# The last SwiGLU on an undivided residual, and an output turned on TensorE

## The chip, the cores and the metric

The kernel runs on one core of one Trainium2 chip. The metric is the device time of one execution in microseconds (us). Engines are named as in the profile: PE is TensorE's matrix multiplication, PEld its weight loads, DVE is VectorE, ACT is ScalarE, SP is SyncE, whose queue issues nearly all DMAs here.

## The reference, cut to what matters

The program is a two-layer backbone over 256 latent tokens and 256 context tokens with 1024 features. Every sub-layer normalises, shifts and scales its input and adds a gated result to the residual. The change touches only the last sub-layer, a SwiGLU over the 256 latent tokens, and the final normalisation:

```python
def rmsnorm(x, g):
    return x * rsqrt(mean(x * x, axis=-1) + 1e-6) * g          # one 1/rms per token

def ffn_half_step(h, m, k, g, w_gate, w_up, w_down):
    shift, scale, gate = m[3 * k], m[3 * k + 1], m[3 * k + 2]   # one number per feature
    hn = rmsnorm(h, g) * (1 + scale) + shift
    return h + 0.5 * gate * ((silu(hn @ w_gate) * (hn @ w_up)) @ w_down)

lat = lat + m[5] * (mixer_output @ w_out)     # end of the odd mixer
lat = ffn_half_step(lat, m, 2, ...)           # w_gate, w_up: 1024 x 2816; w_down: 2816 x 1024
return rmsnorm(lat, final_norm)               # (256 tokens, 1024 features)
```

Since 1/rms is one number per token r(t), hn @ w = r(t) * (x @ w) + shift @ w, where x is the residual times one factor per feature.

## The kernel before

Features lie on the 128 partitions and tokens along the free dimension: the residual `res` is 8 blocks of 128 features by 512 tokens (256 context, 256 latent; `LAT` is the second half). Every product is taken to nearly full precision from halves: `wload` brings a 128x1024 block of weights (512 KB) by a DMA on SP's queue into one of 4 `raw` buffers, ACT rounds it to the high half (L148), DVE subtracts to get the low half (L149), both into one of 4 `w` buffers, and `mm3` (L158, L159, L160) issues three matmuls for each of the contraction's 128-row blocks: high by high, high by low, low by high. Products go to 6 PSUM buffers of 512 columns (`pm`); 2 more (`ps`) serve statistics.

The program is written in order, and a list scheduler sets the order of each engine's queue ahead of time: it takes ready instructions by priority, by its own clock. `high_priority` puts a block's instructions some 100 places earlier, `keep` holds an order as written. On the chip each queue runs in that order: an instruction that waits holds up those behind it.

The stretch around the change runs in these steps:

- **End of the odd mixer.** DVE and ACT finish eight input blocks `os` of the output projection.
- **Output projection** (`out_proj`, which calls `down`): for each of 8 feature blocks, 24 matmuls of 256 columns; DVE adds the gated product to the residual (`residual`, L429), ACT squares it (L291) and DVE adds the square to `acc` (L292).
- **Norm** (`norm_proj` for one half): two matmuls sum `acc` over the partitions (L253), DVE finds 1/rms for 256 tokens, two to a partition (L260 to L269), two matmuls spread it over the partitions (L278), and for each feature block DVE multiplies the residual by 1/rms and by scale (L309), ACT adds the shift and writes the high half (L314), DVE writes the low half (L316). Only then can the block's matmuls begin.
- **SwiGLU** (`ffn`): 22 hidden blocks, each with 24 matmuls for the gate and 24 for the up product, all 256 columns wide; ACT takes silu from PSUM (L458), DVE multiplies with the up product (L459), and ACT and DVE split the result in halves (L164, L165). After 6, 14 and 22 hidden blocks `down` multiplies what there is with w_down and adds to the residual.
- **Output** (`final`): again sums, 1/rms and its spreading, then for each feature block one DVE instruction (L1266) and one DMA of 128 KB on SP's queue (L1269). The output leaves as [feature, token] and is turned on the host.

Of the kernel before, what the change touches and what calls it, by code (L numbers as in the profile page):

```python
# [9 lines left out]
F32 = mybir.dt.float32  # L10
F32R = mybir.dt.float32r
I32 = mybir.dt.int32
AF = mybir.ActivationFunctionType
ALU = mybir.AluOpType
# [4 lines left out]
P = 128  # L19
D = 1024  # L20
KT = D // P
NTOK = 256
T2 = 2 * NTOK
F = 2816
NF = F // P
CHUNKS = ((0, 6), (6, 14), (14, 22))
# [7 lines left out]
SOON = 100  # L34
# [13 lines left out]
CTX, LAT = (0, NTOK), (NTOK, T2)  # L48
# [17 lines left out]
class Builder:  # L66
    def __init__(self, tc, ctx, t, out):
        self.tc, self.nc, self.t, self.out = tc, tc.nc, t, out
        pool = lambda name, bufs, **kw: ctx.enter_context(tc.tile_pool(name=name, bufs=bufs, **kw))
        self.cst = pool("cst", 1)  # L70
        self.rawp = pool("rawp", 4)
        self.wp = pool("wp", 4)
        self.sm = pool("sm", 4)
        self.pmm = pool("pmm", 6, space=PSUM)
        self.psm = pool("psm", 2, space=PSUM)
        self.dram = pool("dram", 1, space=DRAM)
        self.n = 0
        self.bg = []
        self.stage = None
        self.last_act = None  # L80
        self.keep = tc.keep_in_program_order

    def uid(self, s):
# [15 lines left out]
    def small(self, shape, tag, dt=F32, bufs=4):  # L99
        return self.sm.tile(shape, dt, tag=tag, name=self.uid(tag), bufs=bufs)  # L100
# [325 lines left out]
    def residual(self, i, ps, gate, h, last):  # L426
        c0, c1 = h
        r = self.res[:, i, c0:c1]
        self.nc.vector.scalar_tensor_tensor(  # L429
            r, ps[:, c0:c1], gate[:, i, VEC[h] : VEC[h] + 1], r, op0=ALU.mult, op1=ALU.add  # L430
        )
        if last:
            self.stat(i, h)


    def blocks(self, idx, n=3):
# [2 lines left out]
    def ffn(self, l, k, halves, after=None, spare=None, lead=None):  # L439
        nc, t = self.nc, self.t  # L440
        idx = 2 * l + k // 2
        lo, hi = halves[0][0], halves[-1][1]
        wgu = t["wgu"][idx]
        xs, pss = self.norm_proj(l, k, halves, self.blocks(idx, 4 if lead else 3), lead, spare if len(halves) > 1 else None)
        if lead is not None:
            self.mod_setup()
            self.start(self.mod_job((0, m) for m in (2, 3, 4, 5, 6, 7)), 1.6)
        for f0, f1 in CHUNKS:
            hid = []
            for f in range(f0, f1):  # L450
                for g in range(2):
                    if 2 * f + g == len(pss):
                        pss.append(self.pm())
                        w = self.wload(wgu[f, g], D)
                        self.mm3(pss[-1][:, lo:hi], self.wparts(w, KT), self.parts(xs, lo, hi))
                pg, pu = pss[2 * f : 2 * f + 2]
                s = self.slot("h", [P, 2, T2])
                nc.scalar.activation(s[:, 0, lo:hi], pg[:, lo:hi], AF.Silu)  # L458
                nc.vector.tensor_mul(s[:, 1, lo:hi], s[:, 0, lo:hi], pu[:, lo:hi])  # L459
                hd = self.slot("h", [P, 2, T2], F32R)  # L460
                self.split(hd[:, 0, lo:hi], hd[:, 1, lo:hi], s[:, 1, lo:hi])
                hid.append(hd)
                self.tick(2)
            gate = self.need(l, 3 * k + 2)
            self.down(lambda i: t["wd"][idx, i][:, f0 * P : f1 * P], hid, gate, halves, f1 == NF, f1 - f0, after)

    def proj(self, name, blk, xs, c0, c1):
        w = self.wload(self.t[name][blk], D)
        ps = self.pm()
        self.mm3(ps[:, c0:c1], self.wparts(w, KT), self.parts(xs, c0, c1))  # L470
        return ps
# [630 lines left out]
    def odd_mixer(self):  # L1102
        nc, t = self.nc, self.t
# [4 lines left out]
        xs, pss = self.norm_proj(1, 1, both, [t["od_in"][i] for i in ODD], spare="g")  # L1108
# [8 lines left out]
        for i in range(4):  # L1117
            ps = pss[i]
# [17 lines left out]
        for i in range(4):  # L1136
            ps = self.proj("od_in", 16 + i, xs, *LAT)
            nc.scalar.activation(lg[:, i], ps[:, N:T2], AF.Gelu_apprx_tanh)
        gates = {}
        for i in range(4):  # L1140
# [3 lines left out]
            for d in range(2):  # L1144
                ra = gates[i, d] = self.slot("g", [P, 2, T2])
                for g in range(2):
                    ps = self.pm()
# [100 lines left out]
        for i in range(4):  # L1248
            ps = self.pm()
            for f in range(4):  # L1250
                src = (yr if f < 2 else yi)[:, f % 2, i * P : (i + 1) * P]
                nc.tensor.matmul(ps[:, :N], lhsT=src, rhs=idft[:, f, :], start=f == 0, stop=f == 3)
            z = self.slot("hy", [P, N])
            v.scalar_tensor_tensor(z, uu[:, i], hb[:, i : i + 1], ps[:, :N], op0=ALU.mult, op1=ALU.add)
            v.tensor_mul(z, z, x0[:, i])
            o = self.slot("x", [P, 2, T2], F32R)
            self.split(o[:, 0, N:T2], o[:, 1, N:T2], z)
            os.append(o)
        self.out_proj("od_out", 1, os, [LAT])

    def final(self):
        nc = self.nc
        self.rb[LAT] = self.rstd([self.acc[LAT]], self.inv_d)
        for i in range(KT):
            y = self.slot("h", [P, NTOK])
            nc.vector.scalar_tensor_tensor(  # L1266
                y, self.res[:, i, NTOK:T2], self.gain[:, 6, i : i + 1], self.rb[LAT], op0=ALU.mult, op1=ALU.mult
            )
            nc.sync.dma_start(self.out[i], y)  # L1269

    def build(self):
        nc, t = self.nc, self.t
        both = [CTX, LAT]
        self.acc, self.rb, self.mod = {}, {}, {}
        self.res = self.const([P, KT, T2], "res")
        s5p = dict.fromkeys(("sb0", "sb1", "pa", "pb", "bank", "tm", "mb", "mbt", "vt", "et"), 1)
        self.phase(x=8, **s5p, gs=2, sc=1, junk=1, m=2, ct=1, h=10)
        self.ct = self.slot("ct", [P, KT, 32])
        for i in range(0, KT, 2):
            nc.sync.dma_start(self.res[:, i : i + 2, :], t["xt"][:, i : i + 2, :])  # L1280
            if i == 0:
                nc.sync.dma_start(self.ct, t["ct"])
                s5 = self.s5_prepare()
                next(s5)
        nc.scalar.activation(self.ct, self.ct, AF.Silu)
        invs = []
        for n, nm in ((D, "inv_d"), (384, "inv_q"), (256, "inv_kv")):
            tl = self.const([P, 1], nm)
            nc.gpsimd.memset(tl, 1.0 / n)
            invs.append(tl)  # L1290
        self.inv_d, self.inv_q, self.inv_kv = invs
        small = lambda: [
            setattr(self, nm, self.const(shape, nm, t[nm]))
            for nm, shape in (("sel", [P, 2]), ("ident", [P, P]), ("modb", [P, 2, 9, KT]), ("gain", [P, 7, KT]), ("sig", [P, 3]))
        ]
        self.mw0, self.w0 = [], []
        for i in range(KT):
            if i == 6:
                w = self.slot("sc", [P, 2, 4, 2 * P])
                self.mw0.append([w[:, r] for r in range(2)])  # L1300
            else:
                self.mw0.append([self.slot("m" if i == 5 else "h", [P, 4, 2 * P]) for _ in range(2)])
            for r in range(2):
                nc.sync.dma_start(self.mw0[i][r], t["modw0"][i, :, r])
            if i == 0:
                small()
            if i < 2:
                self.w0 += [self.wload(t["wgu"][0, i, g], D) for g in range(2)]
        with self.tc.high_priority(offset=SOON):
            for i in range(KT):  # L1310
                for h in both:
                    self.stat(i, h)
        for m in range(2):
            self.mod[0, m] = self.const([P, KT, 2], f"mraw0_{m}")
        self.start(s5, 2.5)
        self.ffn(0, 0, both, t["ev_in"][EVEN[0]], lead=self.mod_first)
        self.drain()
        self.phase(x=10, hh=2, p=5, c=5, v=2, kr=1, q=8)
        self.even_mixer()
        self.phase(x=8, sc=1, junk=1, m=3, y=7, h=10)  # L1320
        self.mod_setup()
        self.start(self.mod_job(((0, 8),) + tuple((1, m) for m in range(9))), 0.8)
        self.start(self.hyena_prepare(), 0.5)
        self.ffn(0, 2, both, t["wgu"][2, 0, 0], "y")
        self.need(1, 1)
        self.ffn(1, 0, both, t["od_in"][ODD[0]], "h")
        self.drain()
        self.phase(x=8, g=8, lx=2, hy=13)
        self.odd_mixer()
        self.phase(x=8, h=10)  # L1330
        self.ffn(1, 2, [LAT])
        self.final()
        self.stage.close()

# [158 lines left out]
```

## Time and profile before

| | |
|---|---|
| median of 3 runs | 1797.6 us (1797.04 to 1797.97) |
| the profiled execution | 1795.22 us, its span 1793.4 us |
| PE busy | 1727.7 us, 96% of the span |
| PEld, DVE, ACT busy | 81%, 70%, 38% |
| mean granted clock of TensorE | 0.986 of full speed |
| DMA | 292.63 MB, mean 163 GB/s |
| chain that ended last | PE 87%, DVE 7%, DMA 2% |

The span is the time from the first to the last event of one profiled execution; 1.82 us lie around it. [...] PE's records are longer than the distance between their starts, since matmuls overlap: the pace is read from starts.

### The profile page before, as it was taken

The page shows a single profiled execution, that of the slowest core. Times are in us where ns is not written, and L with a number is a line of the kernel's source. Part 1 is how long each engine was busy: PE and PEld are TensorE (multiplying, and loading weights), DVE is VectorE, ACT ScalarE, POOL GpSimd, SP SyncE. Part 2 cuts the span into 40 slices and gives each one's busy share as a digit, 9 for nine tenths or more (in the row PEclk, how much of TensorE's full clock was granted, in tenths as well). Part 3 has the DMA queues.
Part 4 walks back from the last instruction along what each step waited for, and adds up shares of the span by engine and source line. Part 5 has one row for each costly group of instructions (what it writes and reads, how often), then busy time and mean ns, then how long its engine had stood idle before and what let it go on. Part 6 is the DMA issues. An engine that isn't in the chain of part 4 may idle for free.

```text
span 1793.4 us, 24725 instructions
## 1 busy us (share of the span) xinstructions
PE 1727.7 (96%) x9364; PEld 1444.7 (81%) x9364; DVE 1252.9 (70%) x2464; ACT 684.1 (38%) x1082; POOL 13.2 (1%) x47
## 2 busy tenths in 40 slices
PE   5999999999989999999999999999999999789997
PEld 3778777779868788778888888888888888589997
DVE  7999999987488668776666686544543576875555
ACT  4433333343445653222222233222122357554442
POOL 0000000000000000000000000000000000000000
PEclk9999999999998999999999999999999999799999
DMA  9566666652465453464454544555433225146552
GB/s 324 173 216 211 223 214 216 210 189 90 125 185 172 120 189 115 154 223 152 147 183 153 164 130 130 179 173 163 156 117 95 94 94 201 49 150 191 183 185 92
DMA packets 108055, 292.63 MB, mean 163 GB/s; under 512 B 21216, under 2 KB 36448, under 8 KB 107680
## 3 DMA queue, kind: packets, MB, share of 16 engines
q1 hardware_dynamic: 102368, 287.39, 49.8%
q10 hardware_dynamic: 4928, 2.10, 0.7%
q8 instruction: 73, 1.20, 0.3%
q0 software_dynamic: 640, 1.57, 0.3%
q14 instruction: 46, 0.38, 0.1%
HBM read 272.20 MB, written 18.28 MB: 162 GB/s over the span
## 4 chain that ended last, share of the span: by engine, by line
PE 87%; DVE 7%; DMA 2%; ACT 1%; issue 1%; SPq 1%; DVEq 0%; ACTq 0%
PE mm L158 25%; PE mm L160 25%; PE mm L159 25%; PE mm L155 6%; DVE w L149 1%; DMA h<-in_modw_dram 1%; PE mm L1148 1%; SPq L981 1%; DVE nt L309 1%; DMA x<-d_g 1%; DVE x L316 1%; DMA x<-d_v 0%; PE ps L278 0%; PE ps L631 0%; PE ps L1059 0%
## 5 line engine op out<-in xcount | busy, mean ns | idle before, releaser
L159 PE MATMUL mm<-x,w 128*128 128x512 f32 (+1 forms) x1600 | 575.1, 360 | 0.0
L160 PE MATMUL mm<-x,w 128*128 128x512 f32 (+1 forms) x1600 | 574.5, 360 | 0.0
L158 PE MATMUL mm<-x,w 128*128 128x512 f32 (+1 forms) x1600 | 569.4, 361 | 4.5 <-ACT x L314 3.3
L148 ACT CAST w<-raw 128x1024 fp32r<-128x1024 f32 (+2 forms) x324 | 328.5, 1018 | 527.7 <-issue 254.1
L149 DVE TENSOR_TENSOR w<-raw,w 128x1024 fp32r<-128x1024 f32 (+2 forms) x324 | 384.0, 1187 | 191.7 <-ACT w L148 190.8
L158 PEld LDWEIGHTS mm<-x,w 128*128 128x128 f32 x1600 | 300.9, 189 | 55.9 <-ACT x L314 3.9
L159 PEld LDWEIGHTS mm<-x,w 128*128 128x128 f32 x1600 | 301.8, 189 | 48.9 <-issue 2.0
L160 PEld LDWEIGHTS mm<-x,w 128*128 128x128 f32 x1600 | 301.8, 189 | 48.7 <-issue 1.2
L225 DVE CUSTOM_DVE_ANT_0 junk<-m,sc 128x1024 f32<-128x1024 f32 x224 | 273.3, 1220 | 1.8 <-DMA m<-in_modw_dram 0.2
L158 PE MATMUL mm<-h,w 128*128 128x512 f32 (+1 forms) x632 | 229.2, 367 | 0.0
L160 PE MATMUL mm<-h,w 128*128 128x512 f32 (+1 forms) x632 | 228.4, 364 | 0.0
L159 PE MATMUL mm<-h,w 128*128 128x512 f32 (+1 forms) x632 | 228.3, 363 | 0.0
L429 DVE SCALAR_TENSOR_TENSOR res<-mm,mraw,res 128x256 f32<-128x256 f32 x192 | 86.1, 480 | 103.7 <-PE mm L160 92.8
L459 DVE TENSOR_TENSOR h<-h,mm 128x512 f32<-128x512 f32 (+1 forms) x88 | 54.6, 621 | 128.5 <-PE mm L160 111.0
L458 ACT ACTIVATE h<-mm 128x512 f32<-128x512 f32 (+1 forms) x88 | 48.0, 545 | 234.5 <-PE mm L160 223.7
L159 PEld LDWEIGHTS mm<-h,w 128*128 128x128 f32 x632 | 119.1, 188 | 20.6 <-issue 1.0
L158 PEld LDWEIGHTS mm<-h,w 128*128 128x128 f32 x632 | 118.6, 188 | 21.0 <-issue 1.1
L160 PEld LDWEIGHTS mm<-h,w 128*128 128x128 f32 x632 | 118.9, 188 | 20.5 <-issue 0.6
L155 PE MATMUL mm<-x,w 128*128 128x256 f32 x384 | 66.1, 289 | 6.7 <-DVE x L316 6.2
L314 ACT ACTIVATE x<-nt,mraw 128x256 fp32r<-128x256 f32 x88 | 42.9, 506 | 54.5 <-DVE nt L309 54.5
L155 PEld LDWEIGHTS mm<-x,w 128*128 128x128 f32 x384 | 53.9, 188 | 11.6 <-DVE x L316 9.2
L165 DVE TENSOR_TENSOR h<-h,h 128x512 fp32r<-128x512 f32 (+1 forms) x88 | 54.5, 619 | 0.0
(345 smaller groups left out, 1604.5 us busy)
## 6 DMA issues: line engine op xcount, KB each, us to landing
raw<-in_wgu_dram SPq DMA_DIRECT2D x176, 512.0 KB, 3.8
m<-in_modw_dram SPq DMA_DIRECT2D x130, 512.0 KB, 4.3
raw<-in_wd_dram SPq DMA_DIRECT2D x64, 512.0 KB, 3.6
raw<-in_wd_dram SPq DMA_DIRECT2D x32, 384.0 KB, 3.3
raw<-in_od_in_dram SPq DMA_DIRECT2D x20, 512.0 KB, 3.5
h<-in_modw_dram SPq DMA_DIRECT2D x12, 512.0 KB, 9.9
raw<-in_ev_in_dram SPq DMA_DIRECT2D x10, 512.0 KB, 3.5
d_mb<-mbt SPq DMA_DIRECT2D x16, 256.0 KB, 2.9
```

The lines of the kernel that those rows point to most:

```text
L148: nc.scalar.copy(hi[:, :n], raw[:, :n])
L149: nc.vector.tensor_sub(lo[:, :n], raw[:, :n], hi[:, :n])
L155: mm = lambda *a, **k: self.keep(self.nc.tensor.matmul(*a, **k))
L158: mm(ps, lhsT=wh, rhs=xh, start=first and i == 0, stop=False)
L159: mm(ps, lhsT=wh, rhs=xl, start=False, stop=False)
L160: r = mm(ps, lhsT=wl, rhs=xh, start=False, stop=last and i == n - 1)
L165: self.nc.vector.tensor_sub(lo, src, hi)
L225: nc.vector.tensor_tensor_reduce(self.junk, w, self.sc[:, v, :], 1.0, 0.0, ALU.mult, ALU.add, raw[:, dt, v : v + 1])
L314: self.last_act = nc.scalar.activation(x[:, 0, c0:c1], y, AF.Identity, bias=b)
L429: self.nc.vector.scalar_tensor_tensor(r, ps[:, c0:c1], gate[:, i, VEC[h] : VEC[h] + 1], r, op0=ALU.mult, op1=ALU.add)
L458: nc.scalar.activation(s[:, 0, lo:hi], pg[:, lo:hi], AF.Silu)
L459: nc.vector.tensor_mul(s[:, 1, lo:hi], s[:, 0, lo:hi], pu[:, lo:hi])
```

## The change

`ffn_last` takes the place of `ffn` for the last SwiGLU, without `norm_proj`. Its input tiles `xl` hold the residual times the factor per feature, not divided by the rms, in halves, and two more columns that hold the shift. `unscaled` writes the two columns ahead of the output projection, and, through the hook `done` at the end of `residual`, the 256 others as each feature block of the residual is finished: one ACT and one DVE instruction each. Every gate and up matmul is 258 columns wide, so that column 256 of the product is shift @ w. As a product leaves PSUM, it is multiplied by 1/rms (`rb`, spread as before and copied to SBUF once) and gets column 256 as a bias. The gate product: a DVE copy of one column, a DVE multiply, silu with a bias on ACT. The up product: a DVE copy, a DVE multiply, one DVE instruction that adds the bias and multiplies by the gate. The split follows as before.

In the last `down`, the hook of `final_tiles` has ACT multiply each finished residual block by the final gain and TensorE turn it in two 128x128 transposes into 4 PSUM tiles, held from there on. `final` needs 1/rms as one number per partition then, so it is not spread: two DVE and two ACT instructions of 512 columns, each followed by a DMA of 256 KB, two on SP's queue and two on ACT's. The pools of the mixer are kept, with no new phase.

```diff
@@ residual
         if last:
             self.stat(i, h)
+            if self.done is not None:
+                self.done(i, h)
@@
+    def ffn_last(self, l, k, xs):
+        nc, t = self.nc, self.t
+        idx = 2 * l + k // 2
+        n = NTOK
+        with self.tc.high_priority(offset=SOON):
+            rb = self.slot("g", [P, n])
+            nc.scalar.copy(rb, self.rstd([self.acc[LAT]], self.inv_d))
+        gate = self.need(l, 3 * k + 2)
+        for f0, f1 in CHUNKS:
+            hid = []
+            for f in range(f0, f1):
+                pg, pu = self.pm(), self.pm()
+                for g, ps in enumerate((pg, pu)):
+                    w = self.wload(t["wgu"][idx, f, g], D)
+                    self.mm3(ps[:, : n + 2], self.wparts(w, KT), self.parts(xs, 0, n + 2))
+                b = self.small([P, 2], "bias")
+                s = self.slot("g", [P, 2, n])
+                nc.vector.tensor_copy(b[:, 0:1], pg[:, n : n + 1])
+                nc.vector.tensor_mul(s[:, 0, :], pg[:, :n], rb)
+                nc.scalar.activation(s[:, 0, :], s[:, 0, :], AF.Silu, bias=b[:, 0:1])
+                nc.vector.tensor_copy(b[:, 1:2], pu[:, n : n + 1])
+                nc.vector.tensor_mul(s[:, 1, :], pu[:, :n], rb)
+                nc.vector.scalar_tensor_tensor(s[:, 1, :], s[:, 1, :], b[:, 1:2], s[:, 0, :], op0=ALU.add, op1=ALU.mult)
+                hd = self.slot("x", [P, 2, T2], F32R)
+                self.split(hd[:, 0, n:T2], hd[:, 1, n:T2], s[:, 1, :])
+                hid.append(hd)
+            if f1 == NF:
+                self.done = self.final_tiles()
+            self.down(lambda i: t["wd"][idx, i][:, f0 * P : f1 * P], hid, gate, [LAT], f1 == NF, f1 - f0)
+
+    def unscaled(self, l, k, xs):
+        nc = self.nc
+        sh, sc = self.mod[l, 3 * k], self.mod[l, 3 * k + 1]
+        def done(i, h):
+            x, r, g = xs[i], self.res[:, i, h[0] : h[1]], sc[:, i, 0:1]
+            with self.tc.high_priority(offset=SOON):
+                nc.scalar.activation(x[:, 0, :NTOK], r, AF.Copy, scale=g)
+                nc.vector.scalar_tensor_tensor(x[:, 1, :NTOK], r, g, x[:, 0, :NTOK], op0=ALU.mult, op1=ALU.subtract)
+        for i, x in enumerate(xs):
+            self.split(x[:, 0, NTOK : NTOK + 2], x[:, 1, NTOK : NTOK + 2], sh[:, i, 0:1].to_broadcast([P, 2]))
+        return done
@@ odd_mixer
+        self.xl = [self.slot("hy", [P, 2, T2], F32R) for _ in range(KT)]
+        self.done = self.unscaled(1, 2, self.xl)
         self.out_proj("od_out", 1, os, [LAT])
+        self.done = None
+
+    def final_tiles(self):
+        nc = self.nc
+        self.fin = [[self.pm() for _ in range(2)] for _ in range(2)]
+        def done(i, h):
+            y = self.slot("g", [P, NTOK])
+            nc.scalar.activation(y, self.res[:, i, h[0] : h[1]], AF.Copy, scale=self.gain[:, 6, i : i + 1])
+            for j in range(2):
+                nc.tensor.transpose(self.fin[j][i // 4][:, i % 4 * P : (i % 4 + 1) * P], y[:, j * P : (j + 1) * P], self.ident)
+        return done
 
     def final(self):
         nc = self.nc
-        self.rb[LAT] = self.rstd([self.acc[LAT]], self.inv_d)
-        for i in range(KT):
-            y = self.slot("h", [P, NTOK])
-            nc.vector.scalar_tensor_tensor(
-                y, self.res[:, i, NTOK:T2], self.gain[:, 6, i : i + 1], self.rb[LAT], op0=ALU.mult, op1=ALU.mult
-            )
-            nc.sync.dma_start(self.out[i], y)
+        _, r = self.rstd_stats([self.acc[LAT]], self.inv_d)
+        for j in range(2):
+            for q in range(2):
+                y = self.slot("g", [P, T2])
+                if q:
+                    nc.scalar.activation(y, self.fin[j][q], AF.Copy, scale=r[:, j : j + 1])
+                else:
+                    nc.vector.tensor_scalar(y, self.fin[j][q], r[:, j : j + 1], None, op0=ALU.mult)
+                (nc.scalar if q else nc.sync).dma_start(self.out[j, :, q * T2 : (q + 1) * T2], y)
@@ build
         self.odd_mixer()
-        self.phase(x=8, h=10)
-        self.ffn(1, 2, [LAT])
+        self.ffn_last(1, 2, self.xl)
         self.final()
```

## Rows read from the trace of the kernel before

**Rows 1.** Page: busy time by engine, and the chain that ended last, by engine.
```profile
PE 1727.7 (96%) x9364; PEld 1444.7 (81%) x9364; DVE 1252.9 (70%) x2464; ACT 684.1 (38%) x1082; POOL 13.2 (1%) x47
...
PE 87%; DVE 7%; DMA 2%; ACT 1%; issue 1%; SPq 1%; DVEq 0%; ACTq 0%
```

**Rows 2.** Windows: stretch, its length, busy time by engine, clock, DMA share, GB/s.
```profile
1580.00:1600.00 20.00, 14.04 (x99) 13.49 (x98) 13.46 (x39) 7.98 (x13) 0.00 (x0) 0.83 0.28 94
1600.00:1620.00 20.00, 20.00 (x171) 20.00 (x170) 12.48 (x16) 11.38 (x18) 0.00 (x0) 1.00 0.53 168
...
1780.00:1794.00 14.00, 2.66 (x20) 2.16 (x18) 6.08 (x25) 0.42 (x1) 0.00 (x0) 0.72 0.23 76
```

**Rows 3.** Timeline of PE, last output projection to first SwiGLU: start, length, work, idle before.
```profile
1583.59 0.28 PE L160 MATMUL mm<-x,w 128*128 128x256 f32 x1
1586.68 0.58 PE L253 MATMUL ps<-inv_d,acc 128*128 128x1 f32 x4 [2.82 <-DVE acc L292]
...
1591.62 1.23 PE L158 MATMUL mm<-x,w 128*128 128x256 f32 x4 [1.11 <-ACT x L314]
```

**Rows 4.** Timeline of PE: 59 steps of 256 columns, across the first chunk's end.
```profile
1623.82 0.28 PE L158 MATMUL mm<-x,w 128*128 128x256 f32 x1
...
1630.82 0.28 PE L160 MATMUL mm<-h,w 128*128 128x256 f32 x1
```

**Rows 5.** Timeline of PE: 13 steps of 512 columns, an earlier SwiGLU.
```profile
1404.76 0.40 PE L159 MATMUL mm<-h,w 128*128 128x512 f32 x1
...
1407.77 0.40 PE L160 MATMUL mm<-h,w 128*128 128x512 f32 x1
```

**Rows 6.** Timeline of PE: two transposes (L1197) among matmuls, odd mixer.
```profile
1500.84 0.28 PE L158 MATMUL mm<-x,w 128*128 128x256 f32 x1
1500.96 0.38 PE L1197 MATMUL ps<-ident,hy 128*128 128x128 f32 x2
1501.09 0.37 PE L159 MATMUL mm<-x,w 128*128 128x256 f32 x1
1501.30 0.28 PE L160 MATMUL mm<-x,w 128*128 128x256 f32 x1
```

**Rows 7.** Groups by line and shape from 1590 to the end: busy, mean ns, idle before.
```profile
L159 PE MATMUL mm<-x,w 128*128 128x256 f32 x352 | 99.3, 283 | 0.0
...
L149 DVE TENSOR_TENSOR w<-raw,w 128x1024 fp32r<-128x1024 f32 x56 | 68.3, 1225 | 45.9 <-ACT w L148 45.9
...
L429 DVE SCALAR_TENSOR_TENSOR res<-mm,mraw,res 128x256 f32<-128x256 f32 x24 | 11.3, 481 | 16.4 <-PE mm L160 16.2
L459 DVE TENSOR_TENSOR h<-h,mm 128x256 f32<-128x256 f32 x22 | 9.3, 421 | 11.3 <-PE mm L160 6.0 <-ACT h L458 5.0 <-issue 0.3
...
L314 ACT ACTIVATE x<-nt,mraw 128x256 fp32r<-128x256 f32 x8 | 4.0, 507 | 7.7 <-DVE nt L309 7.7
```

**Rows 8.** Timeline of DVE: last residual of the output projection, and what follows.
```profile
1583.90 0.48 DVE L429 SCALAR_TENSOR_TENSOR res<-mm,mraw,res 128x256 f32<-128x256 f32 x1 [0.20 <-PE mm L160]
1584.98 1.23 DVE L149 TENSOR_TENSOR w<-raw,w 128x1024 fp32r<-128x1024 f32 x1 [0.59 <-ACT w L148]
```

**Rows 9.** Timeline of the end: last residual, the 8 output blocks, their DMA issues.
```profile
1781.37 0.48 DVE L429 SCALAR_TENSOR_TENSOR res<-mm,mraw,res 128x256 f32<-128x256 f32 x1 [1.39 <-PE mm L160]
...
1786.36 3.22 DVE L1266 SCALAR_TENSOR_TENSOR h<-res,gain,ps 128x256 f32<-128x256 f32 x8 [0.73 <-PE ps L278]
1786.87 3.78 SPq L1269 DMA_DIRECT2D out_dram<-h  x8
```

**Rows 10.** Windows of the end, columns as in the second group.
```profile
1790.00:1791.00 1.00, 0.00 (x0) 0.00 (x0) 0.00 (x0) 0.00 (x0) 0.00 (x0) 0.50 0.80 269
1791.00:1792.00 1.00, 0.00 (x0) 0.00 (x0) 0.00 (x0) 0.00 (x0) 0.00 (x0) 0.50 0.46 156
```

**Rows 11.** Groups by line and shape, whole kernel: DVE reading PSUM, 2 and 512 columns.
```profile
L260 DVE TENSOR_SCALAR rs_v<-ps 128x2 f32<-128x2 f32 x10 | 1.6, 160 | 7.1 <-PE ps L253 7.1
...
L1068 DVE TENSOR_SCALAR y<-ps,sig 128x512 f32<-128x512 f32 x1 | 0.8, 751 | 2.3 <-ACT y L1067 2.3
```

More of the change, by code (lines that the diff above doesn't have):

```diff
@@ L1258, in odd_mixer @@
             os.append(o)
+        self.xl = [self.slot("hy", [P, 2, T2], F32R) for _ in range(KT)]
+        self.done = self.unscaled(1, 2, self.xl)
         self.out_proj("od_out", 1, os, [LAT])
+        self.done = None
+    def final_tiles(self):
[7 more added lines that the diff above has]
+        return done
     def final(self):
         nc = self.nc
-        self.rb[LAT] = self.rstd([self.acc[LAT]], self.inv_d)
-        for i in range(KT):
-            y = self.slot("h", [P, NTOK])
-            nc.vector.scalar_tensor_tensor(
-                y, self.res[:, i, NTOK:T2], self.gain[:, 6, i : i + 1], self.rb[LAT], op0=ALU.mult, op1=ALU.mult
-            )
-            nc.sync.dma_start(self.out[i], y)
+        _, r = self.rstd_stats([self.acc[LAT]], self.inv_d)
[7 more added lines that the diff above has]
+                (nc.scalar if q else nc.sync).dma_start(self.out[j, :, q * T2 : (q + 1) * T2], y)
     def build(self):
@@ L1486 @@
         aps[name] = nc.dram_tensor(f"in_{name}_dram", a.shape, mybir.dt.from_np(a.dtype), kind="ExternalInput").ap()
-    out = nc.dram_tensor("out_0_dram", (KT, P, NTOK), F32, kind="ExternalOutput").ap()
+    out = nc.dram_tensor("out_0_dram", (2, P, D), F32, kind="ExternalOutput").ap()
     with tile.TileContext(nc, schedule_with_timeline_sim=True) as tc:
@@ L1491 @@
     got = r.results[0]["out_0_dram"]
-    return np.ascontiguousarray(got.reshape(D, NTOK).T).reshape(1, NTOK, D)
+    return np.ascontiguousarray(got).reshape(1, NTOK, D)
```

## The prediction

> **What bounds the kernel now.** I read the page first. PE is busy for 96% of the span and holds 87% of the chain that ended last [rows 1], so an edit pays where PE stands still or runs at the low clock, and costs where it gives PE more to do. The windows of the last stretch show two such places: 1580 to 1600, where PE is busy for 14.04 of 20 us at a mean clock of 0.83, and the end, where it has 2.66 us of work in 14 [rows 2]. Between them PE is busy throughout at full clock, with DVE at some 60% and the DMA engines at half [rows 2]: the SwiGLU itself is bound by the pace of matmuls.
>
> The pace comes from starts, not from the records. 59 steps of 256 columns take 7.00 us [rows 4], so one takes 0.1186 us. 13 steps of 512 columns take 3.01 us [rows 5], 0.2315 us each. The difference over 256 columns is 0.44 ns a column.
>
> The stall is read on PE's timeline. The last matmul of the output projection starts at 1583.59, so the next could have at 1583.71; the SwiGLU's first starts at 1591.62 [rows 3]. PE stands for 7.9 us but for the two small groups of the norm. From there the SwiGLU has 22 x 48 = 1056 gate and up matmuls (three groups of 352, of which one stands in [rows 7]) and 22 x 8 x 3 = 528 of `down`, 1584 in all. At 0.1186 us they take 187.9 us. They took 189.6: the residual add starts 0.31 us after its block's last matmul (1583.90 against 1583.59 [rows 3, 8]), so the very last started at 1781.06 [rows 9] and was through its step at 1781.18. The 1.7 us over are the low clock after the stall and the feature blocks that arrive one by one. Stall and slow start are 7.9 + 1.7 = 9.6 us: what the first half of the change can win.
>
> **What the change takes away and puts in its place, at the start.** The norm's chain (sums, 1/rms, spreading, three instructions per feature block) leaves PE's way, since the first matmuls need only the undivided residual. That gains up to 9.6 us. Against it:
>
> *Two columns more.* 1056 matmuls x 2 columns x 0.44 ns = 0.9 us. From below it is nothing, if the step of 256 is held by something other than columns; but 0.2315 is 1.95 times 0.1186, so columns set it. From above, no row has 257 to 511 columns; a step as long as that of 512 would add 0.113 us x 1056 = 119 us. I take 0.9, since the two forms lie on a line almost through zero.
>
> *Sums and spreading inside the stream.* They were in the stall; now their eight records push matmuls back. By the transposes below (0.11 us each) that is 0.9 us; by their own 0.58 us for four at the low clock [rows 3], 1.2. I take 0.9.
>
> *The last feature block.* After the projection's last matmul the residual add takes 0.48 us [rows 8], then ACT and DVE write the halves: 0.51 by L314, which also has a pointer operand [rows 7], and 0.48. With the hand-overs that is 1.6 us, and PE has the first seven feature blocks of the first product to do meanwhile, 21 x 0.119 = 2.5 us. But ACT begins a weight cast of about 1 us at the same instant (DVE, after its 0.48, waits 0.59 for it and then takes 1.23 for the low half [rows 8]); behind both, the halves come up to 2 us later. So 0 to 1.1 us. PE's queue also holds the sums: they wait for `acc`, which today keeps PE for 2.82 us [rows 3]; placed too early they hold up the matmuls behind them by up to that.
>
> *1/rms itself* comes about 7 us after the projection's end as it does now, and evictions wait for it. Six PSUM buffers hold six products, 6 x 24 x 0.1195 = 17 us of PE's work: hidden; were there two buffers, PE would wait for about 1.5 us.
>
> *The writes of `xl`* (8 ACT and 8 DVE) move into the projection, where DVE waits 0.20 us for PE and 0.59 for ACT in the block shown, and ACT longer [rows 8]: they fit into these waits, but nearly fill them. I take nothing. The 16 small writes of the shift, about 0.16 us each by the 2-column instruction [rows 11], could fall where DVE is finishing the mixer: 0 to 1.3 us.
>
> *Evictions.* DVE has for one hidden block now 2 x 1.225 + 0.42 + 0.42 = 3.3 us. A second multiply (0.42), a three-operand instruction (0.48) and two copies (0.16 each) make 4.5 [rows 7, 11]. PE needs 48 x 0.1195 = 5.7 us: covered by 1.2 us. ACT stays under 3 us. At a chunk's end the chain from the last product to the halves grows by about 0.7 us, and the four PSUM tiles held for the transposes leave two in the last `down`: 0 to 0.6 us.
>
> For all these waits (last feature block, sums, shift writes, chunk ends) the ends are 0 and 5.8 us; I take 1.1, near the low end, because the order is laid out by readiness and PE has other ready matmuls at each of them.
>
> **The end.** 16 transposes: 14 of them lie among the last block's matmuls. In the odd mixer two of them lengthen the time from 1500.84 to 1501.30 to 0.46 us, where two plain steps take 0.237 [rows 6]: 0.11 us each, 1.6 us for 14. The other two run while DVE works on 1/rms. [...]
>
> What is left is the tail after PE. Now 1/rms is there at 1785.6, spread by 1786.36, the first DMA is issued at 1786.87, and the data flow at 269 GB/s into the last window, which is used for about half [rows 9, 10]. After, spreading goes (0.7 us), and the first block of 512 columns takes 0.75 us [rows 11] instead of 0.48: the first issue is about 0.4 us sooner. The megabyte still needs 3.9 us at 269 GB/s, and the producers are quicker (two engines, 1.4 us against 3.2), so the gain lies between 0.4 and 1.0. I take 0.6. [...]
>
> **Sum.** 9.6 - 0.9 - 0.9 - 1.6 + 0.6 - 1.1 = 5.7 us. Against its own time the profiled execution would go from 1795.2 to 1789.5; the median of the runs shown is 2.4 us above that execution, so I predict 1797.6 - 5.7 = 1791.9.
>
> **Rivals.**
> 1. *PE waits inside the stream for what it waited for in the open.* Sums, spreading and the last feature block stand in PE's queue ahead of matmuls that could run. For it: `acc` comes 2.8 us late behind a weight cast [rows 3, 8]. Against: the block of seven ready feature blocks. With 2.8 + 1.1 us more the gain is about 2: 1795.6, no measurable change. Chance 0.16.
> 2. *A transpose costs its whole record.* Two merged records span 0.38 us [rows 6], at 0.11 apart 0.27 each; if a matmul had to wait out each, 14 x 0.16 = 2.2 us more: 1794.1. Against it stand the same rows. Chance 0.04. [...]
> 3. *DVE becomes the pace of the SwiGLU (slower).* In its queue each low half waits for ACT, 45.9 us over 56, 0.82 each [rows 7]. If these waits stay as they are, DVE needs 4.5 + 2 x 0.82 = 6.1 us a hidden block against PE's 5.7, 0.4 x 22 = 8.9 us: 1800.8. It decides once DVE's waits in a hidden block exceed 1.2 + 5.7/22 = 1.5 us. Against: a queue that falls behind finds its inputs ready, and 4 weight buffers give slack. Chance 0.07.
> 4. *258 columns cost more than two columns (slower).* From 5.7 / 1056 = 5.4 ns per matmul over the 0.88 the gain is gone; 10 ns would give 1802.5. No row speaks for it. Chance 0.05.
> 5. *Hardly any cost shows*: without waits and with a tail gain of 1.0 it is 7.2 us, 1790.4; with the two columns free 1789.5. That is within my forecast. A gain above 9 us would need the end of the mixer to be reordered for the better as well: 0.04.
>
> **How the numbers follow.** The forecast itself (a gain of 3.6 to 9 us) has 0.64. This kernel's measurement can tell 0.2%, 3.6 us. Faster: 0.64 + 0.04 = 0.68. Same: rivals 1 and 2, 0.20. Slower: rivals 3 and 4, 0.12. The range leaves out rivals 3 and 4 and the few per cent with a gain above 10: 1787.5 to 1797.5.
>
> **What the profile after would show.** No stall of PE between projection and SwiGLU and a clock of 1.00 there; matmul steps of 0.1195 us; records of L253 and L278 and of the transposes spaced by 0.11 us among matmuls, with no idle time ahead of them; DVE at 75 to 80% in the SwiGLU, still waiting for others; a tail of about 11.4 us from the last matmul instead of 12.2. The prediction is wrong if PE idles in front of sums, transposes or the last feature block by more than 2 us in all, or if the steps grow by over 3 ns.

## The result, and the profile after

The changed kernel takes 1769.2 us (median of 4 runs, 1767.26 to 1772.87) where the kernel before takes 1797.3 (1796.6 to 1797.97): a ratio of 0.9846, interval 0.9829 to 0.9863. The gain of 28 us is five times the forecast of 5.7, and lies outside the stated range. The page after:

```profile
span 1767.9 us, 24860 instructions
...
PE 1704.0 (96%) x9376; PEld 1444.1 (82%) x9376; DVE 1268.6 (72%) x2546; ACT 693.7 (39%) x1101; POOL 13.2 (1%) x47
```

PE has 12 instructions more than in [rows 1] and is busy 23.7 us less. That is the first sign that the gain is not the stall's 8 us: time in which PE stands still is no part of its busy time. Where it was won shows on PE's timeline. The transposes of the odd mixer (L1247 here, [rows 6] before) belong to code that nobody changed: they are PE's instructions 7,322 and 7,323, and the first 7,622, by tiles and shapes, stand in the same order in both kernels:

```profile
1209.65 0.39 PE L161 MATMUL mm<-x,w 128*128 128x512 f32 x1
...
1213.95 0.39 PE L159 MATMUL mm<-x,w 128*128 128x512 f32 x1
...
1477.41 0.38 PE L1247 MATMUL ps<-ident,hy 128*128 128x128 f32 x2
```

They start at 1477.41, not 1500.96: 23.55 us were won before anything that the diff names has run. The first two rows are 19 steps of 512 columns apart (a step is the time from one start to the next), 0.2263 us each, where [rows 5] gave 0.2315. Over all steps of 512 columns the means are 232.2 and 226.9 ns; 4,784 x 5.3 ns = 25.4 us. The 1,536 steps of 256 columns ahead of the last SwiGLU grow by 0.7 ns each, 1.1 us, which leaves 24.3.

The stretch of the change itself, on the same timeline:

```profile
1559.44 0.28 PE L161 MATMUL mm<-x,w 128*128 128x256 f32 x1
1559.56 0.28 PE L159 MATMUL mm<-hy,w 128*128 128x258 f32 x1
...
1566.94 0.28 PE L160 MATMUL mm<-hy,w 128*128 128x258 f32 x1
1567.05 0.50 PE L254 MATMUL ps<-inv_d,acc 128*128 128x1 f32 x4
1567.41 0.37 PE L161 MATMUL mm<-hy,w 128*128 128x258 f32 x1
...
1577.16 0.60 PE L279 MATMUL ps<-ident,rs_y 128*128 128x128 f32 x4
...
1577.72 0.28 PE L161 MATMUL mm<-hy,w 128*128 128x258 f32 x1
1578.68 0.39 PE L159 MATMUL mm<-hy,w 128*128 128x258 f32 x1 [0.68 <-DVE g L490]
...
1734.33 0.44 PE L1323 MATMUL mm<-ident,g 128*128 128x128 f32 x2 [1.89 <-ACT g L1321]
...
1741.80 0.28 PE L159 MATMUL mm<-x,w 128*128 128x256 f32 x1
1741.92 0.38 PE L1323 MATMUL mm<-ident,g 128*128 128x128 f32 x2
1742.06 0.37 PE L160 MATMUL mm<-x,w 128*128 128x256 f32 x1
1742.26 0.28 PE L161 MATMUL mm<-x,w 128*128 128x256 f32 x1
...
1748.19 0.44 PE L1323 MATMUL mm<-ident,g 128*128 128x128 f32 x2 [1.27 <-ACT g L1321]
```

The stall of [rows 3] is gone: projection and SwiGLU are one step apart (1559.44, 1559.56), and the sums at 1567.05 stand among matmuls without a wait. Two transposes lengthen two steps (1741.80 to 1742.26) to 0.46 us, as in [rows 6]. But two other pairs in the stream wait for ACT.

### The profile page after: what moved, and what is told of

Read it like the earlier page. It is cut to its first block, busy times and chain, and to the rows that moved or that the text cites. A ratio compares the mean times of both kernels' runs of the same rounds, so it can differ in the third digit from the quotient of the medians.

```text
span 1767.9 us, 24860 instructions
## 1 busy us (share of the span) xinstructions
PE 1704.0 (96%) x9376; PEld 1444.1 (82%) x9376; DVE 1268.6 (72%) x2546; ACT 693.7 (39%) x1101; POOL 13.2 (1%) x47
## 5 line engine op out<-in xcount | busy, mean ns | idle before, releaser
L160 PE MATMUL mm<-x,w 128*128 128x512 f32 (+1 forms) x1424 | 520.9, 366 | 0.1
L161 PE MATMUL mm<-x,w 128*128 128x512 f32 (+1 forms) x1424 | 520.1, 366 | 0.0
L159 PE MATMUL mm<-x,w 128*128 128x512 f32 (+1 forms) x1424 | 515.4, 367 | 3.6 <-ACT x L315 2.2
L159 PEld LDWEIGHTS mm<-x,w 128*128 128x128 f32 x1424 | 267.8, 189 | 49.3 <-ACT x L315 2.5
L160 PEld LDWEIGHTS mm<-x,w 128*128 128x128 f32 x1424 | 268.9, 189 | 44.5 <-issue 2.0
L161 PEld LDWEIGHTS mm<-x,w 128*128 128x128 f32 x1424 | 268.7, 189 | 43.7 <-issue 1.2
L159 PE MATMUL mm<-h,w 128*128 128x512 f32 x456 | 178.5, 395 | 0.0
L161 PE MATMUL mm<-h,w 128*128 128x512 f32 x456 | 177.1, 391 | 0.0
L160 PE MATMUL mm<-h,w 128*128 128x512 f32 x456 | 176.9, 390 | 0.0
L462 DVE TENSOR_TENSOR h<-h,mm 128x512 f32<-128x512 f32 x66 | 45.3, 687 | 107.6 <-PE mm L161 95.4
L461 ACT ACTIVATE h<-mm 128x512 f32<-128x512 f32 x66 | 39.5, 598 | 195.9 <-PE mm L161 185.2
L159 PEld LDWEIGHTS mm<-h,w 128*128 128x128 f32 x456 | 85.7, 188 | 18.8 <-issue 1.1
L160 PEld LDWEIGHTS mm<-h,w 128*128 128x128 f32 x456 | 85.7, 188 | 18.4 <-issue 1.0
L161 PEld LDWEIGHTS mm<-h,w 128*128 128x128 f32 x456 | 85.6, 188 | 18.4 <-issue 0.6
L159 PE MATMUL mm<-hy,w 128*128 128x258 f32 x352 | 99.4, 284 | 0.7 <-DVE g L490 0.7
L161 PE MATMUL mm<-hy,w 128*128 128x258 f32 x352 | 99.8, 284 | 0.0
L160 PE MATMUL mm<-hy,w 128*128 128x258 f32 x352 | 99.7, 284 | 0.0
```

The costliest lines, as they stand in the source:

```text
L159: mm(ps, lhsT=wh, rhs=xh, start=first and i == 0, stop=False)
L160: mm(ps, lhsT=wh, rhs=xl, start=False, stop=False)
L161: r = mm(ps, lhsT=wl, rhs=xh, start=False, stop=last and i == n - 1)
```

## Experiments

**Is it the change, or its addresses?** The change's new tag `bias` takes 4 tiles of 32 bytes from the pool of small tiles. The pools of `x`, `g`, `h` and `hy` lie above it and move up by 128 bytes (`x` from 97376 to 97504 within a partition), while `w` below stays at 53728 (the addresses that the two programs give their tiles). Theory: this shift shortens the step. Rival: the change does it, by its order. One kernel has the shift without the change, the other the change without the shift:

```diff
# pad128: before, in an unused tag of the small pool (1 and 2 tiles: pad32, pad64)
+        for _ in range(4):
+            nc.vector.memset(self.small([P, 2], "pad", bufs=4), 0.0)
# after_noshift: after, the bias in one more column of s (whose other uses end at n)
-                b = self.small([P, 2], "bias")
-                s = self.slot("g", [P, 2, n])
+                s = self.slot("g", [P, 2, n + 1])
+                b = s[:, :, n]
```

> The kernel before with four unused 32-byte tiles at the end of the small pool, which moves every tile of the later pools (x, h, g, hy and so on) up by 128 bytes, as the new bias tiles of the change do; the queues hold the same instructions in the same order, with four memsets of two columns more on DVE. Theory A (the addresses of the streamed tiles set the step of a matmul): the 512-column step falls from 232 ns to 227 and the time to 1772 to 1776. Theory B (something else of the changed program, or the scheduler): within 2 us of 1797, step 232.

> The changed kernel with the two bias columns kept in two more columns of the s tile instead of tiles of their own, so that all pools lie where they lay before the change. Theory A: the 512-column step is 232 ns again, and what is left is the gain of the changed instructions alone, 4 to 8 us: 1789 to 1794. Theory B: 1767 to 1772 as the changed kernel.

> The kernel before with one unused 32-byte tile: later pools move by 32 bytes. Theory A: the step may differ from 232 ns either way, and the time follows by 4850 matmuls of 512 columns times the difference. Theory B: within 2 us of 1797.

> The kernel before with two unused 32-byte tiles: later pools move by 64 bytes. Theory A: as for 32 bytes, and with the two others a row that shows from which offset on the step changes. Theory B: within 2 us of 1797.

| kernel | x - w, mod 256 bytes | step of 512 | step of 256 (`down`) | us | ratio to before |
|---|---|---|---|---|---|
| before | 128 | 232.2 ns | 118.7 ns | 1797.6 | 1 |
| pad32 | 160 | 234.0 | 117.3 | 1802.7 | 1.0025 (1.0016 to 1.0035) |
| pad64 | 192 | 233.1 | 113.3 | 1789.4 | 0.9956 (0.9942 to 0.997) |
| pad128 | 0 | 226.9 | 120.0 | 1774.0 | 0.9864 (0.985 to 0.9879) |
| after_noshift | 128 | 232.2 | 119.0 | 1796.5 | 0.999 (0.9981 to 1.0) |

128 bytes that nothing uses win 23.6 us; the change at the old addresses wins 1.1, which is no measurable change. The rival fell. But the theory's time for after_noshift, 1789 to 1794, was missed too: it left more to the change alone than the change wins there. "x - w, mod 256" is the distance from the weights to the stream, as the remainder after division by 256. The steps are means over all starts of a kernel's trace, gaps left out.

**What of the addresses?** step_map runs matmuls alone, with the stream and the weights each moved in steps of bytes, and nothing else of the reference's computation. The question is whether the address of the stream alone counts, or that of the weights with it.

> Matmuls alone: the kernel loads one block of streamed data and one of weights, then issues products of 24 matmuls as in the kernel (high by high, high by low, low by high, 8 blocks), with nothing else running, and steps the start of the streamed data through 16 offsets of 32 bytes and that of the weights through 0, 32, 128 and 256; first 512 columns, then 256. It leaves out the whole computation of the reference. [...] Theory N (the address of the stream alone): rows for different weight offsets are alike. [...]

It takes 949 us. Worked out from the starts, 43 steps a point:

```
stream - weights, mod 256     0      32     64     96    128    160    192    224
512 columns, ns a step     226.7  233.3  228.9  233.5  233.4  234.2  233.4  233.2
256 columns, ns a step     120.0  117.7  117.8  119.9  118.6  118.7  117.8  118.3
```

With the weights moved by 0, 32, 128 and 256 bytes (for 256 columns by 0 and 32) the same values come back at the same distances, to 0.3 ns in nearly all points (the largest difference is 1.1 ns), and they repeat after 256 bytes. So Theory N fell: with matmuls alone the step went with the distance between the two operands (226.7 ns for 512 columns at 0, 233.4 at 128), not with one address. Two kernels test that in place: both128 moves `w` and `x` together by 128 bytes, w128 moves `w` by 128 and `x` by 512.

```diff
# both128 and w128: before, a tile of 128 bytes below all pools
+        nc.vector.memset(self.const([P, 32], "padc"), 0.0)
# w128 as well: 384 bytes between w and x
+        nc.vector.memset(self.small([P, 96], "pad", bufs=1), 0.0)
```

> The kernel before with 128 unused bytes among the constants: weights and streamed tiles move up together by 128 bytes, so that the streamed tiles lie where they lie after the change and the weights do not. [...] Theory N: 227 ns, 1774 within 3.

> The kernel before with 128 unused bytes among the constants and 384 in the small pool: weights move by 128 bytes, streamed tiles by 512. [...] Theory N modulo 512: 232 ns and 1797 within 3.

One run each: both128 has the old distance and takes 1796.8 us, w128 adds 384 to the old remainder of 128, which makes 512 or a distance of 0, and takes 1774.3 (before on the same chip 1797.8). PE's timeline of both128, 18 steps:

```profile
1209.84 0.40 PE L158 MATMUL mm<-x,w 128*128 128x512 f32 x1
...
1214.04 0.40 PE L158 MATMUL mm<-x,w 128*128 128x512 f32 x1
```

and of w128, 19 steps:

```profile
1209.76 0.39 PE L159 MATMUL mm<-x,w 128*128 128x512 f32 x1
...
1214.06 0.39 PE L160 MATMUL mm<-x,w 128*128 128x512 f32 x1
```

0.2333 against 0.2263 us in these stretches, at addresses that both differ from those of before. Theory N had it the other way round, 227 ns for both128 and 232 for w128, and fell here too: for steps of 512 columns it is the distance.

**What does the change itself win?** Its halves one by one at the new addresses, beside pad128 and after once more, on one chip; end_half ran on another, and its ratio is to before there. start_half keeps the old `final`. end_half is pad128 with the new `final` and the hook. after_late issues each pair of transposes one feature block later.

```diff
# start_half: after, with final and the output as before
-            if f1 == NF:
-                self.done = self.final_tiles()
# end_half: pad128, in ffn
+            if f1 == NF and halves == [LAT]:
+                self.done = self.final_tiles()
# after_late
-            for j in range(2):
-                nc.tensor.transpose(...)        # of block i
+            ys.append(y)
+            if i:
+                turn(i - 1)
+            if i == KT - 1:
+                turn(i)
```

> The kernel before moved by 128 bytes, again, as the base for the three others on one chip: 1773 to 1775, 0.986 of the kernel before.

> The changed kernel, again. Theory S (beside the move, the change is worth what the prediction summed, less the waits that its trace shows): 4 to 6 us under the moved kernel before, so 1768 to 1770. Theory L (the move is all of it): within 1 us of the moved kernel.

> The changed SwiGLU with the end of the kernel before (1/rms spread, 8 DVE instructions and 8 DMAs, no transposes), at the moved place. Theory S: the stall of 9.6 us goes, 0.9 for sums and 0.3 to 0.9 for two columns come back: 6 to 8 us under the moved kernel, 1766 to 1768, so faster than the whole change, because 14 transposes and the waits for them (1.6 + 3.2 us) cost more than the shorter tail gives (1.8). Theory L: within 1 us of the moved kernel.

> The kernel before with four unused tiles of 32 bytes (so the phase pools stand 128 bytes higher, as in the changed kernel) and with the new end alone: y by row statistics, 16 transposes on TensorE, 1/rms as a per-partition factor, two DMAs; the SwiGLU is the old one, with the stall ahead of it. Theory (the step of 512 columns comes back with the 128 bytes, and the end costs what the two traces of the changed kernel with and without it differ by): against the padded kernel (1774.0) it is 1 to 4 us slower, some 1776 to 1778, with TensorE waiting for ScalarE's y in front of the transposes and a tail shorter by 1.5 to 2 us. Rival (the end costs nothing or gains, as the prediction had it without the waits: 14 transposes of 0.11 against a shorter tail): 1773 to 1774. Second rival (the end costs less at the head of a stalled stage, as the waits are hidden by the old layout of the stream): 1772 to 1774 with no idle time ahead of the transposes.

> The changed kernel with the two transposes of a feature block issued one block later, behind the matmuls of the next. If TensorE's waits for the final-gain tiles (1.9 and 1.3 us in the trace) are lost time, they go: 2.5 to 3.5 us under the changed kernel, 1765 to 1767. If they only moved a wait from elsewhere: within 1 us of it.

From PE's starts: "stall" is from the last matmul of the projection to the SwiGLU's first, "tail" from the start of its last to the span's end.

| us | stall | SwiGLU | tail | median | ratio to before |
|---|---|---|---|---|---|
| before | 8.03 | 189.43 | 12.39 | 1798.0 | 1 |
| pad128 (again) | 8.04 | 191.60 | 12.85 | 1774.0 | 0.9866 (0.9852 to 0.9879) |
| after (again) | 0.12 | 197.61 | 10.71 | 1768.7 | 0.9836 (0.9823 to 0.985) |
| start_half | 0.12 | 192.66 | 12.38 | 1765.8 | 0.9819 (0.9806 to 0.9833) |
| end_half | 8.24 | 199.14 | 10.70 | 1779.5 | 0.9896 (0.988 to 0.9913) |
| after_late | 0.12 | 197.63 | 10.69 | 1768.9 | 0.9841 (0.9827 to 0.9854) |

The first half wins 8.2 us against pad128, and the second loses: 5.5 alone (across two chips; 1 to 4 were expected), 2.8 on top of the first. after_late wins nothing back. In after PE waits twice for ACT within the stream, 1.9 and 1.3 us; in after_late once, but for longer (us, times, longest; the second, of 1.3, comes after the last matmul, as one does in after too):

```profile
PE mm L1323 <- ACT g L1327: 3.9, 2, 2.6
```

And behind that wait the clock fell, which it did not in after (1.00 over the same 20 us; window with clock and DMA share behind POOL, as in [rows 2]):

```profile
1720.00:1740.00 20.00, 17.39 (x136) 17.19 (x135) 11.59 (x19) 8.72 (x14) 0.00 (x0) 0.91 0.44 131
```

So one wait was saved, and the longer one with its low clock took it back.

Most of why end_half loses more by the same wait is seen in its windows:

```profile
1740.00:1742.00 2.00, 0.22 (x2) 0.02 (x1) 1.10 (x2) 1.70 (x3) 0.00 (x0) 1.00 0.79 217
1742.00:1744.00 2.00, 1.88 (x14) 1.89 (x15) 0.60 (x1) 0.06 (x1) 0.00 (x0) 0.83 0.11 45
1744.00:1746.00 2.00, 2.00 (x11) 2.00 (x11) 0.00 (x0) 0.00 (x0) 0.00 (x0) 0.50 0.00 0
1746.00:1748.00 2.00, 2.00 (x16) 2.00 (x16) 0.48 (x1) 1.04 (x2) 0.00 (x0) 0.81 0.00 0
```

and in those of after, round its first wait:

```profile
1732.00:1734.00 2.00, 0.43 (x2) 0.22 (x2) 0.90 (x2) 1.49 (x3) 0.00 (x0) 1.00 0.71 201
1734.00:1736.00 2.00, 1.67 (x14) 1.68 (x15) 0.81 (x1) 0.27 (x1) 0.00 (x0) 1.00 0.15 61
```

From the product's last matmul ahead of the wait to its first behind it, 2.37 us pass in both, but in end_half the clock then falls for a while (0.83, 0.50 and 0.81 in three stretches of 2 us; by an estimate from these, 0.17 + 0.50 + 0.19 of 2 us, 1.7 us of work lost), in after it stays at 1.00. Another 1.1 us lie in end_half's start, where the stall (0.2 us) and the slow steps behind it (0.9 us) come to more than in pad128. Why the clock fell in end_half and not in after is open.

**The tail, and the stream's own start.** after_oneq puts all four output DMAs on SP's queue; start_col48 is start_half with the streamed columns at 48 to 305 of their tiles instead of 0 to 257 (hidden blocks: 48 to 303 instead of 256 to 511), so that no pool moves.

```diff
# after_oneq
-                (nc.scalar if q else nc.sync).dma_start(...)
+                nc.sync.dma_start(...)
# start_col48: OFF = 48 at every write and read of xl and hd
-                    self.mm3(ps[:, : n + 2], self.wparts(w, KT), self.parts(xs, 0, n + 2))
+                    self.mm3(ps[:, : n + 2], self.wparts(w, KT), self.parts(xs, OFF, OFF + n + 2))
```

> The changed kernel with all four output DMAs of 256 KB on SP's queue. Theory (larger DMAs, rows of 2 KB instead of 1 KB, made the output flow at 373 to 379 GB/s where it was 269): the rate stays above 350 GB/s and the tail from the last matmul's start stays within 0.3 us of 10.7. Rival (the second queue made it): the rate goes back to some 270 GB/s and the tail grows by about 1 us, to 11.7.

> The kernel with the first half of the change alone (1765.8), where the streamed tiles of the last SwiGLU, both the residual in halves and the hidden blocks, hold their columns from column 48 on instead of 0 and 256: no tile and no pool moves, but the stream starts 192 bytes later, so at a distance of 192 from the weights (mod 256) instead of 0. Theory 1 (the distance between stream and weights sets the step, wherever it comes from, and the size is that of the kernel with 64 bytes of padding, 113.3 ns per step of 256 columns): some 6.7 ns less for 1584 matmuls, 10.6 us, to 1755. Theory 2 (the same, with the size of the matmuls measured by themselves, 117.8 ns): 2.2 ns x 1584 = 3.5 us, to 1762. Rival (it is where the pools stand, not the stream's own first address): no change, 1765 to 1767, with steps of 120.8 and 120.0.

SP's timeline at after_oneq's end (one run, 1768.4 us):

```profile
1761.29 1.81 SPq L1337 DMA_DIRECT2D out_dram<-g  x4
```

and the window that follows:

```profile
1763.00:1764.00 1.00, 0.00 (x0) 0.00 (x0) 0.00 (x0) 0.00 (x0) 0.00 (x0) 0.50 1.04 389
```

389 GB/s from one queue, and a tail of 10.67 us, where after with two queues has 379 and 10.7: the second queue had no part in it, at 256 KB a DMA. What is left of the two rivals is the larger DMA, 256 KB in rows of 2 KB. What of it counts was not tested, but the rows point to the pace of issues and not to the length of a row: before, SP's queue needs 3.78 us for 8 issues [rows 9], 0.47 each, and 128 KB every 0.47 us are 277 GB/s, near the 269 that flowed, with the DMA engines at a share of 0.80 [rows 10]; here 4 issues need 1.81 us, 256 KB every 0.45 us would be 579 GB/s, and the engines are at 1.04.

start_col48 takes 1763.8 us (1761.0 to 1765.1; ratio 0.9813, 0.98 to 0.9827), by its median the fastest here, though its interval overlaps start_half's; its SwiGLU is 3.6 us shorter (189.07). `down` on start_half's timeline, 13 steps:

```profile
1737.73 0.28 PE L159 MATMUL mm<-x,w 128*128 128x256 f32 x1
...
1739.29 0.28 PE L160 MATMUL mm<-x,w 128*128 128x256 f32 x1
```

and on start_col48's, 14 steps:

```profile
1737.77 0.28 PE L162 MATMUL mm<-x,w 128*128 128x256 f32 x1
...
1739.36 0.28 PE L161 MATMUL mm<-x,w 128*128 128x256 f32 x1
```

120.0 against 113.6 ns here, 113.4 over all of `down`: 528 x 6.6 ns = 3.5 us, with no tile or pool moved. So the stream's own first address counts, and the rival of the pools fell. But the 1056 steps of 258 columns stayed at 120.7 to 120.8, which neither theory had. Theory 1 expected 10.6 us and got a third. Theory 2 expected 3.5 us and got them by luck: 2.2 ns on all 1584 steps, where the trace has 6.6 on a third of them and next to nothing on the rest.

## Why the prediction was wrong

**The step that failed** is the sum's: "Against its own time the profiled execution would go from 1795.2 to 1789.5". It adds up the stretch that the diff names and takes the pace of all other matmuls, "13 steps of 512 columns take 3.01 us, 0.2315 us each", as a property of the kernel that an edit elsewhere can't touch. It is one of the addresses: 128 bytes that nothing uses took the mean step from 232.2 to 226.9 ns (pad128). The last matmul of the projection starts 24.2 us earlier (1583.59, 1559.44); from there to the end the two profiled executions differ by 1.4 us (209.85, 208.45). Rival 5 held that "A gain above 9 us would need the end of the mixer to be reordered for the better as well"; PE's order there is the old one, and the gain came all the same.

That 1.4 is what is left of the change against a SwiGLU that the move itself makes slower: a step of 256 columns goes from 118.7 to 120.0 ns, and pad128 takes 212.5 us from that point to the end. At equal addresses, after against pad128, the change's own terms can be read:

| term | predicted | in the trace |
|---|---|---|
| stall and slow start | 9.6 | 7.9 + 1.7 = 9.6 |
| two columns | -0.9 | -0.6 (start_half: -0.9) |
| sums, spreading | -0.9 | -0.9 |
| transposes | -1.6 | -1.3 |
| waits | -1.1 | -4.9 |
| tail | 0.6 | 2.2 |
| sum | 5.7 | 4.1 |

The spans of these two executions differ by 3.9, the medians by 4.8 to 5.3. So at the new addresses the size of the sum was nearly right, but by luck: waits 3.8 us too small stand against a tail, columns and transposes that came out 2.2 us better. The prediction's own sign of being wrong, PE idle for "more than 2 us in all" in front of sums, transposes or the last feature block, came true: 1.9 + 1.3 us in front of transposes.

- *Stall and slow start* went as predicted: no idle time at 1559.5, and the clock stays at 1.00 in the windows of after. pad128's SwiGLU takes 191.63 us for 1583 steps of 0.120, so 1.67 were the slow start.

```profile
1540.00:1560.00 20.00, 20.00 (x169) 20.00 (x168) 14.93 (x27) 12.47 (x22) 0.00 (x0) 1.00 0.48 147
1560.00:1580.00 20.00, 19.32 (x161) 19.11 (x160) 13.20 (x39) 8.75 (x11) 0.00 (x0) 1.00 0.57 189
...
1620.00:1640.00 20.00, 20.00 (x169) 20.00 (x169) 15.21 (x29) 10.03 (x15) 0.00 (x0) 1.00 0.55 184
```

- *Two columns* cost 120.84 - 120.01 = 0.83 ns in start_half, 0.88 predicted. At the old addresses (after_noshift) a step of 258 takes 121.2 against 118.7, 2.7 us for 1056: one reason why the change wins less there (the spans differ by 2.8 us). Rival 4 was right that columns can cost more than their share, with a smaller price.
- *Sums, spreading, transposes* cost 0.11 us each among matmuls: four sums lengthen two steps by 0.44 us, a pair of transposes by 0.22; 12 of the 16 lie in the stream, not 14. Rival 2 fell: a transpose's record is 0.27 us long (0.38 - 0.11), more than twice what it costs.
- *Waits* were taken "near the low end, because the order is laid out by readiness", and that was wrong: 0.95 us at 1577.72 and 4.0 in the last `down`. The first comes of another step that failed, "*1/rms itself* comes about 7 us after the projection's end as it does now": `acc` was complete at 1563.1, but the sums ran at 1567.05, 1/rms was ready at 1575.0, behind four weight splits of 1.2 us on DVE, and was spread at 1577.16, 17.7 us after that end. By then the products had used up "6 x 24 x 0.1195 = 17 us" of PSUM buffers, and PE waited for DVE. The 4.0 are rival 1's mechanism with another culprit: not the sums, but the transposes, in a queue that runs in order, ahead of matmuls that could run (the weights of those behind the first wait had been split by 1731.53; they start at 1734.52). At the first wait ACT is behind:

```profile
1732.51 1.04 ACT L149 CAST w<-raw 128x1024 fp32r<-128x1024 f32 x1 [1.81 <-PE mm L161]
1733.46 0.41 ACT L288 ACTIVATE acc<-res 128x256 f32<-128x256 f32 x1
1733.78 0.49 ACT L1321 ACTIVATE g<-res,gain 128x256 f32<-128x256 f32 x1
```

  A weight cast, then the square for the sums, and only then the block that the transposes wait for. At the second, 1748.19, no cast lies between: residual add, square and product follow the block's last matmul, and PE waits for all three. DVE did not become the pace (15.2 of 20 us above): rival 3 fell.
- *The tail* is 10.7 us; "the megabyte still needs 3.9 us at 269 GB/s" failed. Its timeline after:

```profile
1762.51 0.97 ACTq L1337 DMA_DIRECT2D out_dram<-g  x2
1762.52 1.00 SPq L1337 DMA_DIRECT2D out_dram<-g  x2
```

and a window of it:

```profile
1764.00:1765.00 1.00, 0.00 (x0) 0.00 (x0) 0.00 (x0) 0.00 (x0) 0.00 (x0) 0.50 1.04 379
```

  The first issue comes 5.3 us after the last matmul's start, 5.8 in [rows 9], which is the predicted 0.4 and a little; in pad128, the base of the table, it comes after 6.3. The rest, 1.1 to 1.2 us, is the rate: 379 GB/s against 269 [rows 10].

## What to carry to other kernels

Before an edit's time is put down to its idea, run the old kernel with the new tiles allocated and unused: here they were worth 23.6 of 28 us, and half of the change cost time. In a kernel bound by the pace of matmuls, compare the step between starts in a stretch that the edit does not touch (here 0.2315 and 0.2263 us); if it moved, look at the distance between the addresses of the stream and of the weights. In after, transposes that waited for ACT kept PE for 1.9 and 1.3 us in front of its other work, with ACT busy for only 39% of the span: the engine that PE waits for needs to be free at that moment, not on the average. That such a piece of work belongs behind work that is ready is the author's inference and was not shown: one block later was not enough here (1768.9 us against 1768.7), and no run placed it better.

## What the runs showed of the hardware

With weights loaded for each matmul (4704 of each in step_map), the step went with the distance between the streamed operand and the weights modulo 256 bytes: 226.7 to 234.2 ns for 512 columns, 117.7 to 120.0 for 256 when measured alone. The best distance for the one (0, 226.7 ns) is, with 96, the worst for the other (120.0 and 119.9). Why the distance counts was not shown.

Open is why a step of 256 columns at distance 192 takes 113.3 ns in the kernel (pad64, and start_col48's `down`) but 117.8 alone (at 160 it is 117.3 against 118.7), and why 258 columns stayed at 120.8 there. A kernel with distance 0 for its 512 columns and 192 for all of its 256 was not tried. Behind a wait of PE of 1.9 us the clock fell to 0.50 in end_half and stayed at 1.00 in after; behind one of 2.6 us in after_late it was 0.91 over 20 us. Whether the wait sets the clock was not shown.
